# A 3x3 convolution on one core: all inputs through GpSimd's queue, a 20-row head without fp32 staging, and a first store that waits for the fourth pair

## The chip, the cores and the metric

The kernel runs on one core of a Trainium2 chip. The metric is the device time of one execution in microseconds (us), the median of some runs. Most runs of one kernel agree within 0.3% (126.94 to 127.12 us for the kernel before), so differences of half a percent need several runs beside runs of the kernel before on the same chip. Engines go by the profiler's names: PE multiplies matrices (TensorE) and PEld loads its weights, DVE is VectorE, ACT is ScalarE, POOL is GpSimd and SP is Sync. A DMA packet is one piece of a load or store on one of the 16 DMA engines.

## The reference, cut to what matters

```python
batch, c_in, h, w, c_out, k = 16, 64, 64, 64, 128, 3
# x: (16, 64, 64, 64) fp32, weight: (128, 64, 3, 3) fp32, 90% zeros
x_pad = np.pad(x, ((0, 0), (0, 0), (1, 1), (1, 1)))
output[b, co] += weight[co, ci, kh, kw] * x_pad[b, ci, kh:kh+h, kw:kw+w]   # over ci, kh, kw
```

The input is 16.8 MB, the weights are 0.29 MB and the output is 33.6 MB, all fp32. The kernel treats the weights as dense.

## The kernel before

Two images make a pair, whose 2 x 64 channels fill the 128 partitions; there are eight pairs. The products are taken in bf16. The loads on GpSimd's queue turn the inputs into bf16 on their way into the core; only the first 32 rows of pair 0 (the "head") come in fp32 by Sync's queue and are then cast by VectorE and ScalarE. For part of the rows GpSimd adds neighbouring rows first, and PE uses the sum for both ("sums" below). ACT and DVE copy PE's results out ("evacuation").

```python
w_sb = const_pool.tile([C_OUT, C_IN * KH * KW], FP32, name="w_sb")
nc.sync.dma_start(out=w_sb, in_=weight.rearrange("o i kh kw -> o (i kh kw)"))
x_head = o_pool.tile([128, H, W], FP32, name="o")
nc.sync.dma_start(out=x_head[:, 0:HEAD, :], in_=pair(0)[:, 0:HEAD, :])        # HEAD = 32
nc.gpsimd.dma_start(out=xs[0][:, HEAD:H, :], in_=pair(0)[:, HEAD:H, :])
ident = const_pool.tile([128, 128], BF16, name="ident")
make_identity(nc, ident)
def load(p):
    nc.gpsimd.dma_start(out=xs[p], in_=pair(p))
EARLY = 4
for p in range(1, EARLY):
    load(p)
# ... filling matmuls, weight casts and transposes on PE, cast_x of the head's rows ...
for p in range(NP):
    o = [o_pool.tile([C_OUT, H, W], FP32, name="o") for _ in range(2)]         # 7 buffers
    for blk in range(4):
        ...                        # sums on GpSimd, products on PE, evacuation by ACT and DVE
        if p > 0 and blk == 1 and p + EARLY - 1 < NP:
            load(p + EARLY - 1)
    for n in range(2):
        nc.sync.dma_start(out=out[2 * p + n], in_=o[n])                        # last pair: in halves
```

## Time and profile before

| | before |
|---|---|
| time, median of 4 runs | 127.04 us |
| HBM read and written | 17.07 + 33.55 MB |
| first DMA packet, last DMA packet | 1.76, 123.95 us |
| first product of PE, end of its stream of products | 7.43, 111.1 us |
| stores alone, 72 to 114 us | 426 GB/s |

The time is about 3.4 us longer than the end of the last DMA packet in the profiled execution (127.33 against 123.95 us).

### The profile page before, as it was taken

To read this page: it belongs to the slowest core of one execution; us is meant where nothing else is said; L and a number is where in the kernel's file an instruction comes from. 1 tells how busy PE (TensorE), PEld (TensorE's weight loads), DVE (VectorE), ACT (ScalarE), POOL (GpSimd) and SP (SyncE) were. 2 spreads that over 40 slices of the span, in tenths; PEclk is the share of its full clock that TensorE was granted. 3 is DMA by queue.
4 is the path that set the end of the run, shared out by engine and by line. 5 is a ranking of instruction groups with operands and counts; after the bars stand their busy time and mean duration, and the time that the engine had idled before them with its cause. 6 is when DMAs were issued, how large, how long until landed. Compare 5 with 4: busy or idle time off the path is not lost.

```text
span 125.6 us, 2510 instructions
## 1 busy us (share of the span) xinstructions
PE 109.4 (87%) x1014; PEld 56.1 (45%) x1014; DVE 82.3 (66%) x135; ACT 39.0 (31%) x71; POOL 40.6 (32%) x45
## 2 busy tenths in 40 slices
PE   6769999999999999999999999999999999970000
PEld 6624444545454545444554555455545555430000
DVE  0352477877787777888788878877877787772000
ACT  4541533333333333333333333333333333330000
POOL 6327353334433443334333333333333330000000
PEclk9967999999999999999999999999999999999555
DMA  4999999999999999999999999999999999999980
GB/s 119 361 230 214 214 209 219 217 157 399 423 334 305 303 433 311 344 308 407 342 305 329 397 428 444 418 420 423 438 428 444 418 423 423 433 405 423 431 373 26
DMA packets 4044, 42.93 MB, mean 342 GB/s; under 512 B 448, under 2 KB 448, under 8 KB 704
## 3 DMA queue, kind: packets, MB, share of 16 engines
q1 hardware_dynamic: 2880, 34.90, 66.1%
q0 software_dynamic: 1152, 7.86, 30.9%
q8 instruction: 8, 0.13, 0.4%
q14 instruction: 4, 0.03, 0.1%
HBM read 17.07 MB, written 33.55 MB: 403 GB/s over the span
## 4 chain that ended last, share of the span: by engine, by line
PE 83%; DMA 5%; DVE 1%; issue 1%; DVEq 0%; SPq 0%
PE ps L146 83%; DMA o<-in_x_dram 5%; DVE o L179 1%; DVEq L229 0%; DVE x L97 0%; SPq L60 0%; DVEq L179 0%
## 5 line engine op out<-in xcount | busy, mean ns | idle before, releaser
L179 DVE TENSOR_TENSOR o<-ps,pc 128x512 f32<-128x512 f32 x124 | 77.8, 686 | 22.1 <-PE ps L146 19.8
L146 PE MATMUL ps<-x,wT 64*128 64x504 bf16 (+3 forms) x780 | 90.1, 378 | 1.5 <-DVE x L97 1.5
L146 PEld LDWEIGHTS <-wT 64*128 64x128 bf16 x966 | 52.1, 95 | 54.0 <-issue 3.4
L165 POOL TENSOR_TENSOR s<-x 128x512 bf16<-128x512 bf16 x31 | 35.6, 1151 | 59.7 <-PE ps L146 43.3
L172 ACT COPY pc<-ps 128x512 f32<-128x512 f32 x62 | 33.3, 589 | 64.0 <-issue 61.8
L146 PE MATMUL ps<-s,wT 64*128 64x512 bf16 (+1 forms) x186 | 25.5, 377 | 0.0
L82 PE MATMUL ps<-idle_rhs 128*128 128x128 bf16 x39 | 3.9, 283 | 1.0 <-DVE idle_rhs L77 1.0
L82 PEld LDWEIGHTS <-idle_rhs 128*128 128x128 bf16 x39 | 3.5, 133 | 1.0 <-DVE idle_rhs L77 1.0
L68 POOL DMA_DIRECT2D x<-in_x_dram x7 | 3.9, 559 | 0.0
L160 DVE COPY o<-ps 128x512 f32<-128x512 f32 x2 | 1.4, 692 | 3.6 <-PE ps L146 3.6
L101 DVE CAST w_bf<-w_sb 128x192 bf16<-128x192 f32 (+1 forms) x4 | 1.1, 345 | 2.8 <-DMA w_sb<-in_weight_dram 2.8
L159 ACT COPY o<-ps 128x512 f32<-128x512 f32 x2 | 1.2, 586 | 4.0 <-PE ps L146 4.0
L97 ACT CAST x<-o 128x576 bf16<-128x576 f32 (+1 forms) x2 | 1.5, 802 | 1.2 <-DMA o<-in_x_dram 1.2
L97 DVE CAST x<-o 128x576 bf16<-128x576 f32 x1 | 0.5, 460 | 2.0 <-DMA o<-in_x_dram 2.0
L101 ACT ACT_TABLE_LOAD x1 | 1.3, 1283 | 0.7 <-PEq L218 0.7
L101 ACT CAST w_bf<-w_sb 128x64 bf16<-128x64 f32 (+1 forms) x2 | 0.7, 416 | 1.7 <-DMA w_sb<-in_weight_dram 1.7
L107 PE MATMUL ps<-ident,w_bf 128*128 128x128 bf16 x9 | 0.9, 222 | 0.3 <-DVE w_bf L101 0.3
L111 DVE TENSOR_TENSOR wT<-ps,wT 128x384 bf16<-128x384 f32 x2 | 1.0, 550 | 0.0
L63 POOL DMA_DIRECT2D x<-in_x_dram x1 | 0.7, 691 | 0.8 <-POOLq L218 0.8
L107 PEld LDWEIGHTS <-w_bf 128*128 128x128 bf16 x9 | 0.5, 97 | 0.8 <-DVE w_bf L101 0.7
L77 DVE MEMSET idle_rhs<- 128x64 uint32 x1 | 0.1, 112 | 0.8 <-PEq L218 0.8
L122 DVE CAST wT<-ps 128x384 bf16<-128x384 f32 x1 | 0.6, 552 | 0.0
(8 smaller groups left out, 1.9 us busy)
## 6 DMA issues: line engine op xcount, KB each, us to landing
out_dram<-o SPq DMA_DIRECT2D x14, 2048.0 KB, 16.9
x<-in_x_dram POOLq DMA_DIRECT2D x7, 1024.0 KB, 15.5
out_dram<-o SPq DMA_DIRECT2D x4, 1024.0 KB, 10.6
o<-in_x_dram SPq DMA_DIRECT2D x1, 1024.0 KB, 5.7
x<-in_x_dram POOLq DMA_DIRECT2D x1, 512.0 KB, 7.5
w_sb<-in_weight_dram SPq DMA_DIRECT2D x1, 288.0 KB, 3.0
```

The lines of the kernel that those rows point to most:

```text
L68: nc.gpsimd.dma_start(out=xs[p], in_=pair(p))
L82: nc.tensor.matmul(idle_ps, idle_rhs, idle_rhs, start=True, stop=True)
L97: copy(out=xs[0][:, a:b, :], in_=x_head[:, a:b, :])
L101: copy(out=w_bf4[:, g, a:b, :], in_=w_v[:, k : k + b - a, :])
L107: nc.tensor.matmul(wps[:, j, :], src, ident, start=True, stop=True)
L111: nc.vector.tensor_tensor(out=wT[:, g], in0=wps, in1=wT[:, G1], op=SUB)
L146: nc.tensor.matmul(ps[n][:, lo:hi, c_lo:c_hi], tap(g, kw, n), src[q, a:b:step, c_lo + kw - 1 : c_hi + kw - 1], start=(i == 0), stop=(i == ...
L159: nc.scalar.copy(out=o[0][:, r0 : r0 + rows, :], in_=ps[0])
L160: nc.vector.tensor_copy(out=o[1][:, r0 : r0 + rows, :], in_=ps[1])
L165: nc.gpsimd.tensor_tensor(out=s, in0=xs[p][:, r0 : r0 + 16 : 2, :], in1=xs[p][:, r0 + 1 : r0 + 16 : 2, :], op=ADD)
L172: nc.scalar.copy(out=c, in_=shared[n])
L179: nc.vector.tensor_tensor(out=o[n][:, first : r0 + 16 : 2, :], in0=ps[n], in1=pc[n], op=ADD)
```

## The change

The intent is to put all inputs in one queue in the order in which they are needed, to do without the fp32 staging and its casts, to start PE sooner on a shorter head, and to keep the first stores from competing with the loads that PE needs.

```diff
-    HEAD = 32
+    HEAD = 20
...
+    def load(p, a=0, b=H):
+        return nc.gpsimd.dma_start(out=xs[p][:, a:b, :], in_=pair(p)[:, a:b, :])
     w_sb = const_pool.tile([C_OUT, C_IN * KH * KW], FP32, name="w_sb")
     nc.sync.dma_start(out=w_sb, in_=weight.rearrange("o i kh kw -> o (i kh kw)"))
-    x_head = o_pool.tile([128, H, W], FP32, name="o")
-    nc.sync.dma_start(out=x_head[:, 0:HEAD, :], in_=pair(0)[:, 0:HEAD, :])
-    nc.gpsimd.dma_start(out=xs[0][:, HEAD:H, :], in_=pair(0)[:, HEAD:H, :])
+    load(0, 0, HEAD)
     ident = const_pool.tile([128, 128], BF16, name="ident")
     make_identity(nc, ident)
...
-    EARLY = 4
-    for p in range(1, EARLY):
-        load(p)
+    load(0, HEAD, H)
+    EARLY = 5
+    landed = [load(p) for p in range(1, EARLY)][-2]
...   (cast_x and its three calls go)
-                if p > 0 and blk == 1 and p + EARLY - 1 < NP:
-                    load(p + EARLY - 1)
+                if p > 1 and blk == 1 and p + EARLY - 2 < NP:
+                    load(p + EARLY - 2)
...
-                nc.sync.dma_start(out=out[2 * p + n], in_=o[n])
+                st = nc.sync.dma_start(out=out[2 * p + n], in_=o[n])
+                if p == n == 0:
+                    tc.add_manual_dep(st.ins, landed.ins.name, ..., reason="loads first")
```

More of the change, by code (lines that the diff above doesn't have):

```diff
@@ L58 @@
     xs = [x_pool.tile([128, H, W], BF16, name=f"x{p}") for p in range(NP)]
+    def load(p, a=0, b=H):
+        return nc.gpsimd.dma_start(out=xs[p][:, a:b, :], in_=pair(p)[:, a:b, :])
     w_sb = const_pool.tile([C_OUT, C_IN * KH * KW], FP32, name="w_sb")
     nc.sync.dma_start(out=w_sb, in_=weight.rearrange("o i kh kw -> o (i kh kw)"))
-    x_head = o_pool.tile([128, H, W], FP32, name="o")
-    nc.sync.dma_start(out=x_head[:, 0:HEAD, :], in_=pair(0)[:, 0:HEAD, :])
-    nc.gpsimd.dma_start(out=xs[0][:, HEAD:H, :], in_=pair(0)[:, HEAD:H, :])
+    load(0, 0, HEAD)
     ident = const_pool.tile([128, 128], BF16, name="ident")
     make_identity(nc, ident)
-    def load(p):
-        nc.gpsimd.dma_start(out=xs[p], in_=pair(p))
-    EARLY = 4
-    for p in range(1, EARLY):
-        load(p)
+    load(0, HEAD, H)
+    EARLY = 5
+    landed = [load(p) for p in range(1, EARLY)][-2]
     idle_rhs = const_pool.tile([128, 128], BF16, name="idle_rhs")
@@ L94, in tap @@
         return wT[64 * n : 64 * n + 64, g, (kw - n) % 3, :]
-    def cast_x(copy, a, b):
-        copy(out=xs[0][:, a:b, :], in_=x_head[:, a:b, :])
     def cast(g, copy, a, b):
@@ L118 @@
     cast(G2, nc.vector.tensor_copy, 3, 4)
-    cast_x(nc.vector.tensor_copy, 0, 9)
     nc.scalar.copy(out=wT[:, G1], in_=transposed(G1))
@@ L125 @@
     keep_busy(12)
-    cast_x(nc.scalar.copy, 9, 18)
     difference(G01, ps0)
     difference(G21, ps2)
-    cast_x(nc.scalar.copy, 18, HEAD)
     def product(terms, rows):
@@ L202 @@
             for n in range(2):
-                nc.sync.dma_start(out=out[2 * p + n], in_=o[n])
+                st = nc.sync.dma_start(out=out[2 * p + n], in_=o[n])
+                if p == n == 0:
+                    tc.add_manual_dep(
+                        st.ins,
+                        landed.ins.name,
+                        mybir.DependencyInfo(
+                            mybir.DependencyClass.Sync, mybir.DependencyReason.DATA
+                        ),
+                        reason="loads first",
+                    )
 _INS = ['x', 'weight']
```

## The prediction

> **What bounds the kernel now.** I read the page first, from its slices, then the queues, then the chain of waits.
>
> ```profile
> PE   6769999999999999999999999999999999970000
> DMA  4999999999999999999999999999999999999980
> GB/s 119 361 230 214 214 209 219 217 157 399 423 334 305 303 433 311 344 308 407 342 305 329 397 428 444 418 420 423 438 428 444 418 423 423 433 405 423 431 373 26
> ...
> q1 hardware_dynamic: 2880, 34.90, 66.1%
> q0 software_dynamic: 1152, 7.86, 30.9%
> ...
> HBM read 17.07 MB, written 33.55 MB: 403 GB/s over the span
> ...
> PE 83%; DMA 5%; DVE 1%; issue 1%; DVEq 0%; SPq 0%
> ```
>
> The chain names PE for 83%, and PE is solid from the third slice on. But PE ends four slices before the span does, while the DMA engines are at 9 from the second slice to the second last. A load that converts is counted by the bf16 bytes that land, half of what is read from HBM, so the 214 of the load phase is 428 of reading. Nowhere is there a slack slice on the DMA. So the chain, which stops at the last store, hides the bound: all 16 DMA engines, 66.1 + 30.9 = 97% of the span in the two data queues.
>
> The windows view gives the rates (columns: window, its us, five engines' busy us, clock, DMA share, GB/s):
>
> ```profile
> 24.00:26.00 2.00, 2.00 (x22) 1.03 (x20) 1.40 (x4) 0.44 (x1) 0.62 (x1) 1.00 1.15 205
> 26.00:28.00 2.00, 2.00 (x22) 0.96 (x18) 1.27 (x3) 1.07 (x2) 1.15 (x1) 1.00 0.93 131
> ...
> 72.00:114.00 42.00, 40.30 (x379) 19.98 (x374) 32.65 (x53) 13.39 (x26) 11.05 (x10) 1.00 1.00 426
> 114.00:122.00 8.00, 0.00 (x0) 0.00 (x0) 0.00 (x0) 0.00 (x0) 0.00 (x0) 0.66 0.98 416
> ```
>
> Stores alone run at 426 GB/s. All 50.62 MB at that rate take 118.8 us. The first packet starts near 1.76 us and the last ends near 124 us, so only some 3.4 us of the DMA's stretch are not full-rate transfer: a ragged end of about 1.5 us, a ramp of about half a microsecond at the start, and one dip. The dip is at 24 to 28 us, where the first store enters: the loads' 215 falls to 205 and then 131, and the packets there are twice as long. In 26 to 28 us about 0.9 us of transfer is lost, with the neighbours 1.1 us.
>
> The timeline of the start (start, us, engine, line, what):
>
> ```profile
> 0.74 0.38 SPq L60 DMA_DIRECT2D w_sb<-in_weight_dram  x1
> ...
> 1.18 0.43 SPq L62 DMA_DIRECT2D o<-in_x_dram  x1
> 1.24 0.69 POOL L63 DMA_DIRECT2D x<-in_x_dram  x1 [0.80 <-POOLq L218]
> ...
> 6.92 0.46 DVE L97 CAST x<-o 128x576 bf16<-128x576 f32 x1 [2.02 <-DMA o<-in_x_dram]
> 7.29 0.55 DVE L122 CAST wT<-ps 128x384 bf16<-128x384 f32 x1
> 7.43 5.57 PE L146 MATMUL ps<-x,wT 64*128 64x512 bf16 x36 [1.53 <-DVE x L97]
> ```
>
> PE's first useful product waits until 7.43 us for a cast of the fp32 head, and PE ends its stream at 111.1 us.
>
> **What the Trainium skill says.** Page "DMA: Bandwidth & Descriptors", section "Issuing engines are not separate DMA queues": all issuers share the same 16 engines and interleave. The trace agrees: where both queues are busy the landed stores plus twice the landed loads stay near 428 GB/s. So moving the head from one queue to the other makes no bandwidth. Same page, "Specifications": the first byte takes about 1 us on GpSimd's path, 0.6 us on Sync's. Here the weight load's issue ends at 1.12 us and its first packet starts at 1.76 us, 0.64 us later: agrees. GpSimd's first load is issued at 1.24 us, and its first packet starts only at 5.18 us, 3.9 us later; that seems to contradict the page. Page "Perfetto Trace Analysis", section "DMA Instruction — SWDGE (GPSIMD)": the recorded instruction ends when the last descriptor has been written. Then these descriptors were ready at 1.93 us, and something else held them.
>
> **What held them** is the hinge of this prediction. In the packets, every engine moves its 8 weight packets, its 8 packets of the fp32 head, and then at once, with no gap, its first packet of GpSimd's queue. A late doorbell would have left gaps, or would have cut in between head packets. So GpSimd's packets stood behind work already taken in. The first store looks the same from the other side: issued at 23.5 us, first packet 27.7 us, 4.2 us later, on the queue that needed 1.0 us from the start of the issue when nothing was ahead. I conclude that about 3 us of either delay is what is already in the engines, and that alone, behind only 0.29 MB of weights, GpSimd's first packet starts at 1.93 + 0.7 to 1.0, about 2.7 us.
>
> **The change part by part.**
> 1. *Start of the DMA's stream.* Removed: a 1.05 MB load on Sync's queue. Added: the same bytes on GpSimd's. HBM bytes: unchanged, 50.62 MB. What can change is a hole between weights and head. The weights are finished on the engines between 2.9 and 3.3 us. First packet at 2.7 us: no hole; at 3.5 us: a hole of about 0.4 us; at 5.2 us, if the delay were fixed: about 2.0 us (5.2 less 3.2). Added packet cost: a converting packet of 8 KB takes 322 ns against 309 ns for a plain one, 8 per engine: 0.1 us. I take +0.3 us in all.
> 2. *Start of PE.* The first 20 rows are 0.66 MB; with 0.29 MB of weights 0.95 MB, at 426 GB/s 2.2 us. From an effective start of 2.5 us that is 4.7, plus 0.4 us to the semaphore (head's last packet 6.5 us, cast 6.9 us): 5.1 us. The cast of 0.46 us goes, and so does the wait of the weight cast behind it at 7.29 us. Now the weights' own chain decides: the filling products end at 5.89 us. The weights may land up to 0.4 us later as they share with the head. PE starts at 5.9 to 6.4, about 1.3 us earlier, and its stream ends near 109.8 instead of 111.1 us.
> 3. *The other 44 rows* are 1.44 MB, 3.4 us more: landed near 8.7 us. GpSimd's sum for the second block needs them, takes 1.15 us, and ends near 10 us; PE wants it 5.4 us after its start, at 11.3 us or later. No stall.
> 4. *The store's wait.* Pair 3 was issued at 3.54 us and landed 20.6 us later, at 24.1 us; the first store went at 23.5 us. In the new kernel the bytes up to pair 3 are the same, so it lands near 24.2 us and the store goes some 0.7 us later than before, beside pair 4, which is already queued. The engines have 4.9 us of pair 4 to do meanwhile (2.10 MB at 426), longer than the 4.2 us until a store's first packet. So there is no hole, and the dip stays about as it is. I credit 0.1 us of it.
> 5. *Output buffers.* The head took one of 7. Every pair still waits for the store seven allocations earlier. No PE wait for a store is seen now, and a store stream moved by under 1 us makes none.
> Sum: +0.3 - 0.1 = +0.2 us, so 127.2 us. The 1.3 us of PE is off the path that sets the end: the queue is already some 10 us behind when PE stops (last evacuation 113.7 us, last packet 124 us).
>
> **The rivals.**
> A. *GpSimd's first-packet delay is fixed at about 4 us.* For: 3.9 us here, and about 4.1 us for loads issued at 43.8 and 56.6 us. Against: all had full engines ahead of them, and the store shows the same delay. Then the DMA stands for 2.0 us after the weights, the whole stream moves by that, PE starts near 7.3 as now, and the time is 129.0 to 129.4 us.
> B. *PE sets the end.* For: 83% of the chain, idle only at the start. Then all 1.3 us arrive at the end: 125.7 us. Against: 10 us of transfers after PE's end at full rate.
> C. *The wait cures the dip*: loads are nearly done when stores enter, 1.1 us of transfer comes back, 126.0 us. Against: pair 4 is as much in the way as before.
> D. *Six loads outstanding at the start instead of four* block GpSimd's queue and make its sums late. For: only the four were tried here. Against: PE has slack of over 1 us there and the DMA would run on. About 127.5 us.
>
> **Range and chances.** My own path has 0.65, A in full or in part 0.18, C 0.10, B and D the rest. Centre 127.2 us; range 126.1 to 128.9 us, longer upwards because of A. Faster by 2% needs under 124.5 us, which is less than the ragged end and the dip together can give: 0.03. Slower by 2% needs over 129.6 us, rival A and a hole at the store besides: 0.07. Within 2%: 0.90.
>
> **What would show it right or wrong.** In the new profile: DMA share 9 from the second slice on and the first packet of the software queue before 3.3 us (step 1; rival A if it is after 4.5 us, with a hole in 3 to 5 us); first product on L140 or so at 5.9 to 6.4 us (step 2); no wait of PE for the sums up to 15 us (step 3); first store issued at 24 to 24.6 us, and the 131 GB/s dip 4 us later still there (step 4); no PE wait for stores (step 5); PE's stream over by 110 us and yet the same last packet near 124 us. Wrong altogether would be an end that moves with PE's end, or a mixed phase whose rate differs from 426.

## More of the kernel before

The start of the windows view is needed later (columns: window in us, its length, busy us and instructions of PE, PEld, DVE, ACT and POOL, granted clock, DMA share, GB/s landed); a load that converts lands half of the bytes that it reads, so some 215 is full speed for GpSimd's loads, and some 428 for Sync's.

```profile
3.00:4.00 1.00, 1.00 (x10) 0.79 (x8) 0.24 (x1) 0.24 (x2) 1.00 (x3) 1.00 1.08 413
4.00:5.00 1.00, 0.66 (x9) 0.46 (x9) 0.90 (x4) 0.81 (x3) 0.09 (x1) 1.00 0.94 393
5.00:6.00 1.00, 0.90 (x16) 0.81 (x14) 0.00 (x0) 0.64 (x2) 0.00 (x0) 1.00 0.99 303
6.00:7.00 1.00, 0.00 (x0) 0.00 (x0) 0.08 (x1) 0.08 (x1) 0.00 (x0) 1.00 1.13 225
```

In 3 to 5 us it is Sync's head that lands at about 400, in 5 to 6 us the two queues change over, and from 6 us on GpSimd's loads land at full speed at once.

## The result

| | before | changed |
|---|---|---|
| median | 127.04 us (126.94 to 127.12, 4 runs) | 128.44 us (128.21 to 128.75, 4 runs) |
| ratio of the fast runs | | 1.0112, 95% interval 1.0089 to 1.0136 |
| last DMA packet, profiled execution | 123.95 us | 125.22 us |

A ratio is the mean time of one kernel's fast runs over that of the other's of the same rounds, so it is not quite the ratio of the medians quoted. Executions over 1.5% slower than the fastest of the same kernel are left out of the means. The change costs 1.1%. That is inside the range and within 2%, but 1.2 us above the predicted 127.2 us, and the sign matters to whoever would keep the change.

The page of the changed kernel, the lines that answer to those of before:

```profile
PE   6876999999999999999999999999999999910000
DMA  4999999999999999999999999999999999999960
GB/s 101 129 199 216 225 212 220 212 230 390 405 310 323 336 418 305 312 341 429 315 318 323 421 424 439 436 413 429 434 434 423 423 424 449 423 400 424 424 269 10
...
q1 hardware_dynamic: 2736, 33.85, 63.3%
q0 software_dynamic: 1296, 8.39, 32.8%
HBM read 17.07 MB, written 33.55 MB: 399 GB/s over the span
```

The DMA engines are "busy" just as before, and as many bytes cross HBM. But the second slice landed 129 GB/s. A busy share counts the time that packets take, and slow packets look as busy as quick ones; only the GB/s row beside it shows the loss. The dip that the kernel before has in its ninth slice (157) is gone: the changed kernel has 230 there.

The start of the timeline:

```profile
0.74 0.38 SPq L65 DMA_DIRECT2D w_sb<-in_weight_dram  x1
...
1.24 0.69 POOL L61 DMA_DIRECT2D x<-in_x_dram  x1 [0.79 <-POOLq L221]
...
2.46 2.68 POOL L61 DMA_DIRECT2D x<-in_x_dram  x5
...
7.03 3.99 PE L140 MATMUL ps<-x,wT 64*128 64x512 bf16 x36 [0.90 <-DMA x<-in_x_dram]
...
10.83 3.36 POOL L159 TENSOR_TENSOR s<-x 128x512 bf16<-128x512 bf16 x3 [5.70 <-DMA x<-in_x_dram]
...
12.03 0.82 PE L140 MATMUL ps<-s,wT 64*128 64x512 bf16 x6 [1.01 <-POOL s L159]
```

PE waits for the head until 7.03 us, and then 1.01 us more for GpSimd's sum of the second block, whose rows landed late. Its stream ends at 110.3 us, 0.8 us sooner than before, while the kernel ends later. The windows view of the changed kernel says where the transfers were slow:

```profile
3.00:4.00 1.00, 1.00 (x10) 0.79 (x8) 0.26 (x1) 0.27 (x2) 1.00 (x3) 1.00 0.91 162
4.00:5.00 1.00, 0.77 (x8) 0.55 (x8) 0.89 (x4) 0.65 (x3) 1.00 (x3) 1.00 1.35 134
5.00:6.00 1.00, 1.00 (x17) 0.96 (x15) 0.77 (x2) 0.78 (x2) 0.14 (x1) 1.00 0.80 93
6.00:7.00 1.00, 0.14 (x3) 0.09 (x1) 0.72 (x2) 0.00 (x0) 0.00 (x0) 1.00 0.77 144
...
26.00:28.00 2.00, 2.00 (x22) 1.06 (x20) 1.27 (x3) 0.80 (x2) 0.97 (x1) 1.00 1.05 221
```

Between 4 and 7 us 134, 93 and 144 landed where 215 is full speed. At 26 to 28 us 221 landed where the kernel before had 131. So the two kernels lose transfer time in different places.

**A ledger of lost transfer.** From the packets I summed, for each half microsecond, the HBM bytes that moved, and took what was missing against 428 GB/s as time lost, from 1.5 us on; it includes the wait for the first packet at 1.74 to 1.76 us. To find each engine's last packet I followed the packets from end to start, as the records do not name the engine. Each row is one profiled execution. All in us:

| kernel | time, median | lost by 10 us | lost 22 to 31 us (first stores) | mean of the 16 engines' last packets | the last of them |
|---|---|---|---|---|---|
| before | 127.04 | 1.02 | 1.16 | 122.40 | 123.95 |
| changed | 128.44 | 2.56 | 0.02 | 122.76 | 125.22 |
| e1 no wait | 128.24 | 2.64 | 0.31 | 123.06 | 124.84 |
| e2 head by Sync | 126.82 | 1.67 | 0.10 | 121.92 | 123.46 |
| e3 before + wait | 127.25 | 1.02 | 0.91 | 122.09 | 123.80 |
| e4 one load fewer ahead | 127.98 | 2.64 | 0.01 | 122.89 | 124.53 |
| e5 head 32 rows | 128.61 | 2.10 | 0.17 | 122.48 | 124.91 |
| e6 before + ahead + wait | 127.06 | 1.07 | 0.59 | 122.00 | 123.63 |
| e7 contiguous head | 128.65 | 2.91 | -0.01 | 123.25 | 125.02 |
| e8 pair 0 in one load | 130.24 | 2.09 | 0.12 | 125.32 | 126.87 |
| e9 loads held back | 128.12 | 2.30 | 0.07 | 122.51 | 124.65 |
| e10 filler on Sync | 128.56 | 1.58 | 0.10 | 123.48 | 125.04 |
| e11 before, 20 rows | 127.11 | 1.47 | 0.53 | 122.13 | 123.68 |
| e12 out of step | 127.22 | 1.20 | 0.53 | 122.18 | 124.04 |

The sum checks: changed against before, +1.54 at the start and -1.14 at the first stores are +0.40 us, and the mean of the last packets moved by +0.36 us. The rest is that the slowest engine is 2.46 us behind the mean instead of 1.55, which adds 0.91 us: 125.22 - 123.95 = 1.27 us. In all fourteen profiled executions the time is 3.2 to 3.5 us more than the last packet, so it is the slowest of the sixteen engines that counts. The profiled execution of the changed kernel is its slowest run (128.75 us), so part of the 0.91 us is that run's own. How far one execution can be trusted shows where kernels share a part: with one and the same start the loss repeats (1.02, 1.02 and 1.07 in before, e3 and e6; 2.56, 2.64 and 2.64 in the changed kernel, e1 and e4), and so does the dip with the wait and a 20-row head on GpSimd's queue (0.02, 0.01, -0.01 and 0.07 in the changed kernel, e4, e7 and e9). The lag of the slowest engine does not repeat in these four: 2.46, 1.64, 1.77 and 2.14 us.

How the slowest engine comes to lag shows in the DMA view cut to 118 to 126 us, 0.2 us a column. Of before:

```profile
GB/s 328 492 410 410 492 369 451 451 410 369 532 369 410 451 410 451 410 369 164 287 328 164 287 82 0 41 41 0 41 0 0 0 0 0 0 0 0 0 0 0
```

and of the changed kernel:

```profile
GB/s 451 369 492 451 369 410 451 451 410 451 410 451 328 451 532 287 410 451 328 328 369 287 123 246 123 82 123 0 41 41 0 41 0 41 41 0 0 0 0 0
```

Each kernel fades out from about 121.5 us on, as engine after engine is done, and one engine alone moves the last packets (41 GB/s is one packet of 8 KB in a column); in the changed kernel it does so for longer.

### The profile page after: what moved, and what is told of

Same layout as the page of the kernel before. It is cut to its first block, busy times and chain, and to the rows that moved or that the text cites. A ratio compares the mean times of both kernels' runs of the same rounds, so it can differ in the third digit from the quotient of the medians.

```text
span 126.9 us, 2507 instructions
## 1 busy us (share of the span) xinstructions
PE 108.4 (85%) x1014; PEld 59.5 (47%) x1014; DVE 81.9 (65%) x134; ACT 37.4 (30%) x69; POOL 41.1 (32%) x46
## 4 chain that ended last, share of the span: by engine, by line
PE 77%; DMA 6%; POOL 2%; issue 1%; DVE 1%; DVEq 0%; POOLq 0%
PE ps L140 77%; DMA x<-in_x_dram 6%; DVE o L173 1%; POOL s L159 1%; POOL x L61 1%; DVEq L232 0%; POOL ident masks.py:199 0%; POOL ident masks.py:197 0%; POOLq masks.py:199 0%; POOLq L159 0%; POOLq L221 0%; DVEq L173 0%
## 5 line engine op out<-in xcount | busy, mean ns | idle before, releaser
L140 PE MATMUL ps<-x,wT 64*128 64x504 bf16 (+3 forms) x780 | 88.8, 373 | 0.9 <-DMA x<-in_x_dram 0.9
L140 PEld LDWEIGHTS <-wT 64*128 64x128 bf16 x966 | 55.1, 94 | 49.9 <-DVE o L154 1.3
L61 POOL DMA_DIRECT2D x<-in_x_dram x9 | 5.1, 574 | 0.8 <-POOLq L221 0.8
L116 ACT CAST wT<-ps 128x384 bf16<-128x384 f32 x1 | 0.5, 478 | 0.4 <-PE ps L104 0.4
L120 ACT CAST wT<-ps 128x384 bf16<-128x384 f32 x1 | 0.5, 478 | 0.2 <-PE ps L104 0.2
```

Source lines behind the costliest of these rows:

```text
L61: return nc.gpsimd.dma_start(out=xs[p][:, a:b, :], in_=pair(p)[:, a:b, :])
L140: nc.tensor.matmul(ps[n][:, lo:hi, c_lo:c_hi], tap(g, kw, n), src[q, a:b:step, c_lo + kw - 1 : c_hi + kw - 1], start=(i == 0), stop=(i == ...
```

## The experiments

Three calls of up to four kernels and one of a single kernel, twelve kernels in all. Each call ran beside the kernel before on the same chip: medians 127.17, 127.06, 127.17 and 127.27 us there. The changed kernel itself ran in a call of its own (127.04 us there), so differences to it of 0.2 us or so say little. e1 to e4 were written to tell the parts of the change apart. **Theory 1** was that the start loses the time and the store's wait gives back the dip; the rivals were that the wait itself costs (2), that the dip's absence was chance (3), or that the number of loads queued ahead matters (4).

### e1: the changed kernel without the wait

```diff
-                if p == n == 0:
-                    tc.add_manual_dep(st.ins, landed.ins.name, ..., reason="loads first")
```

> The changed kernel without the first store's wait. Theory 1 (the 1.4 us come from the start, where GpSimd's queue alone feeds the engines and loses about 1.3 us between 4 and 7 us, and the wait gives back the 1.1 us dip that the early first store made): first store near 22 us, the dip of packets twice as long is back near 24 to 28 us, and the time rises to 129.2 to 129.7 us. Theory 2 (the wait itself costs, the store stream starts late): the time falls to 127.0 to 127.6 us. Theory 3 (the wait does nothing, the dip's absence is chance): 128.3 to 128.6 us.

Measured: 128.24 us (127.97 to 128.36). The first store went at 23.13 instead of 25.38 us. The start is as slow as ever (2.64 us lost). The dip came back only to 0.31 us, not to 1.1. Theory 2 falls, as the time did not drop to 127.6 or less. Theory 1 is right on the start and wrong on the wait: the wait is worth about 0.3 us of transfer at the mean, and nothing that the times show. Something else in the change had removed most of the dip.

### e2: the head by Sync's queue again, the rest as changed

```diff
-    load(0, 0, HEAD)
+    x_head = o_pool.tile([128, H, W], FP32, name="o")
+    nc.sync.dma_start(out=x_head[:, 0:HEAD, :], in_=pair(0)[:, 0:HEAD, :])
+    load(0, HEAD, H)
...
+    cast_x(nc.vector.tensor_copy, 0, 9)
...
+    cast_x(nc.scalar.copy, 9, HEAD)
```

> The changed kernel, but the 20 head rows go through Sync's queue in fp32 with casts, as before; loads ahead and wait kept. Theory 1: no stall at 4 to 7 us and no dip at 24 to 28 us, so better than both: 125.9 to 126.5 us. Theory 2 (the wait costs): stays near 128.4 us. Theory 4 (the stall is of six loads queued ahead, whoever loads the head): a stall is still seen at 4 to 8 us and the time stays at 127.5 us or more.

Measured: 126.82 us (126.71 to 126.93), 1.6 us below the changed kernel by this one edit. The windows view of e2:

```profile
4.00:5.00 1.00, 0.75 (x11) 0.53 (x11) 0.83 (x4) 0.81 (x2) 0.61 (x2) 1.00 1.14 279
5.00:6.00 1.00, 0.83 (x15) 0.74 (x13) 0.00 (x0) 0.57 (x2) 0.00 (x0) 1.00 0.90 187
6.00:7.00 1.00, 0.37 (x4) 0.22 (x5) 0.89 (x3) 0.78 (x1) 0.00 (x0) 1.00 1.04 214
...
26.00:28.00 2.00, 2.00 (x22) 1.08 (x20) 2.00 (x4) 0.24 (x1) 0.14 (x1) 1.00 1.06 221
```

By 6 us GpSimd's loads land at full speed (214), and there is no dip (221). The loss by 10 us fell from 2.56 to 1.67 us, not to the 1.02 of before. Theory 4 falls here too: five loads are written on GpSimd's queue by 4.6 us, and yet its stream is at full speed by 6 us. The time is 0.3 us above the upper end of what I had expected (126.5 us). e2 is the quickest kernel: each of its four runs is below each of the seven runs of before (127.01 us and up), though the interval of the ratio, 0.9931 (0.9856 to 1.0007), is wide because two runs of before came out at 128.7 us.

### e3: the kernel before with the wait alone

```diff
-    for p in range(1, EARLY):
-        load(p)
+    landed = [load(p) for p in range(1, EARLY)][-1]
...   (and the wait of the first store on `landed`)
```

> The kernel before, with only the first store's wait for the fourth pair added. Theory 1: the dip at 25 to 28 us shrinks or goes, and the time falls by up to 1.1 us: 126.0 to 126.6 us. Theory 2: 127.5 us or more. Theory 3: 127.0 us with the dip still there.

Measured: 127.25 us median of four runs, fast runs 127.18 to 127.28 and a slow one of 129.37 us. The first store went at 24.34 instead of 23.50 us, and the windows view of e3 has the dip still:

```profile
24.00:26.00 2.00, 2.00 (x22) 1.10 (x20) 1.59 (x3) 0.24 (x1) 0.42 (x1) 1.00 1.04 213
26.00:28.00 2.00, 2.00 (x22) 1.03 (x18) 1.27 (x3) 1.08 (x2) 1.16 (x1) 1.00 1.00 135
```

It only starts later and is a quarter smaller (0.91 against 1.16 us). Theory 3 is nearest: the wait alone does not pay.

### e4: one load fewer ahead

```diff
-    EARLY = 5
-    landed = [load(p) for p in range(1, EARLY)][-2]
+    EARLY = 4
+    landed = [load(p) for p in range(1, EARLY)][-1]
...
-                if p > 1 and blk == 1 and p + EARLY - 2 < NP:
-                    load(p + EARLY - 2)
+                if p > 0 and blk == 1 and p + EARLY - 1 < NP:
+                    load(p + EARLY - 1)
```

> The changed kernel with pairs 1 to 3 ahead instead of 1 to 4, so five loads written at the start instead of six, the fifth pair's in the loop as before. Theory 1: nothing changes, 128.2 to 128.7 us, stall at 4 to 7 us as long. Theory 4 (number of loads queued ahead, or their descriptors being written beside the transfers): the stall is shorter and the time 127.3 to 127.9 us.

Measured: 127.98 us (127.74 to 128.08), between the two theories' numbers. The loss at the start is 2.64 us as in e1, so the load less does not shorten it; the slowest engine lags by 1.64 us here. The number of loads ahead is not the cause.

The next four ask what is slow about the head. **Theory Q**: GpSimd's loads start badly with nothing ahead of them. **Theory P**: pieces of 5 KB cut out of rows of 16 KB are slow to read, by either queue.

### e5: 32 rows instead of 20

```diff
-    HEAD = 20
+    HEAD = 32
```

> The changed kernel with 32 head rows instead of 20, still by GpSimd's queue. In the changed kernel packets took 1.2 us per engine too long between 3 and 7 us. Theory Q (the queue: GpSimd's loads start badly when nothing is ahead of them): the loss stays at 1.0 us or more, time 128.0 to 128.7 us. Theory P (the piece: 5 KB out of every 16 KB row are slow to read, whoever reads them): 8 KB pieces are as quick as they were before, loss 0.4 us or less, time 126.7 to 127.3 us.

Measured: 128.61 us with a wide scatter (127.77 to 129.03). Lost by 10 us: 2.10 us, 0.46 less than with 20 rows, but still 1.08 more than before, with the same 32 rows by Sync. Packets alone took some 0.8 us per engine too long between 3 and 7 us. The time is Q's; the piece's size has a part in it.

### e6: 32 rows by Sync, with loads ahead and the wait

```diff
-    HEAD = 20
+    HEAD = 32
...   (against e2; the head's last rows are cast as before)
```

> 32 head rows by Sync in fp32 as before, but pairs 1 to 4 ahead and the first store's wait, as in the change: it differs from e2 in the 20 rows only, and from e3 in the fourth load's place. Theory P: start as quick as before (loss from 3 to 7 us under 0.3 us against 0.8 in e2). The dip at the first store was 1.16 us before, 0.83 in e3, 0.17 in e2: if it hangs on the fifth load being issued early it is under 0.3 us here and the time is 126.2 to 126.6 us; if it hangs on the 32 rows (engines in step with each other) it is 0.7 us or more and the time 127.0 to 127.3 us.

Measured: 127.06 us (127.01 to 127.66). The start is as quick as before (1.07 us), as P expects of the larger pieces. The dip is 0.59 us, between both expectations: the early fifth load takes 0.3 us off e3's dip, the 20 rows another 0.5. So the wait, the early load and the shorter head each soften the dip, and the head most; the first store goes at 24.49 us here and at 24.50 in e2, so its time is not what differs between the two.

### e7: the same bytes in the same pieces, but contiguous (a wrong result)

```diff
-    load(0, 0, HEAD)
+    flat = x.rearrange("n i h w -> (n i h) w")[0 : 128 * HEAD, :]
+    nc.gpsimd.dma_start(out=xs[0][:, 0:HEAD, :], in_=flat.rearrange("(p h) w -> p h w", h=HEAD))
```

> The changed kernel, whose first load takes as many bytes in the same 128 pieces of 5 KB, but from one contiguous stretch of x: a wrong result on purpose. Theory P (gaps between the pieces, every 16 KB): no loss in the head's own packets, loss from 3 to 7 us 0.5 us or less, time 127.0 to 127.6 us. Theory Q: as the changed kernel, 1.0 us or more and 128.1 to 128.7 us.

Measured: 128.65 us (128.45 to 128.86), 2.91 us lost by 10 us. The gaps between the pieces are not the cause. P falls in this form.

### e8: pair 0 in one load of 64 rows

```diff
-    HEAD = 20
+    HEAD = 64
...
-    load(0, HEAD, H)
```

> The changed kernel with pair 0 in one load of 64 rows by GpSimd's queue: no pieces at all, contiguous 2 MB. PE starts 1.5 us later, near 8.5 us, which is off the path. Theory P: no loss from 3 to 7 us, time 126.6 to 127.2 us. Theory Q: the loss of 1.0 us or more is still there, time 128.0 us or more.

Measured: 130.24 us (129.93 to 130.64). Lost by 10 us: 2.09 us, as in e5, though there are no pieces at all. So GpSimd's start costs 1.07 us more than before whatever the shape (2.10 and 2.09 against 1.02), and Q stands. The time itself went beyond what either theory said, because my expectation of PE was wrong. The chain of e8 (start, us, what):

```profile
1.24 9.73 DMA x<-in_x_dram
...
11.01 104.16 PE ps L139 x954
```

The last engine brought pair 0 at 10.67 us, and PE began at 11.01 instead of 8.5 us. The windows view then shows the engines at a share of 0.88 and 369 GB/s in 102 to 108 us, and summed as for the ledger 2.6 us are lost between 31 and 110 us (0.04 in the changed kernel): stores came too late to keep them busy. PE's slack is real, but 4 us is more than there is.

### e9: fewer descriptors written beside the first transfers

```diff
-    landed = [load(p) for p in range(1, EARLY)][-2]
+    load(1)
+    hold = const_pool.tile([128, 1, 4], BF16, name="hold")
+    nc.gpsimd.tensor_copy(out=hold, in_=xs[0][:, 0:1, 0:4])
+    landed = [load(p) for p in range(2, EARLY)][-2]
```

> The changed kernel, but GpSimd issues the loads of pairs 2 to 4 only once the head has landed (it reads four elements of it first), so that three loads are written at the start instead of six. Theory D (the slow packets of 3 to 7 us come from GpSimd writing further loads' descriptors beside them, 2.5 to 5.1 us): the landed rate from 4 to 7 us, 134, 93 and 144 GB/s in the changed kernel, rises to 180 or more, time 127.2 to 127.7 us. Theory R (a stream of GpSimd's loads with nothing ahead of it needs some 4 us to come to speed, whatever is issued behind): rates as in the changed kernel, 128.0 to 128.7 us.

Measured: 128.12 us (127.51 to 128.19). The windows view of e9:

```profile
4.00:5.00 1.00, 1.00 (x14) 0.79 (x14) 0.80 (x4) 0.71 (x2) 0.00 (x0) 1.00 1.01 124
5.00:6.00 1.00, 0.64 (x12) 0.56 (x10) 1.00 (x3) 0.48 (x1) 0.00 (x0) 1.00 0.93 176
6.00:7.00 1.00, 0.74 (x8) 0.42 (x9) 0.33 (x1) 0.00 (x0) 0.73 (x3) 1.00 0.91 175
```

The rates of 5 to 7 us rose from 93 and 144 to 176 and 175, but 4 to 5 us stayed at 124, after GpSimd had stopped writing at 3.5 us; and when the held loads were written (6.4 to 8.0 us) some 0.3 us were lost between 7.5 and 9 us. In all 0.26 us less was lost. That is the net: by the packets 0.5 us less was lost from 3 to 7 us, and 0.3 us more from 7 to 9.5 us, where the writing now was. So the writing (D) may cost up to a third of the 1.54 us where it falls, though a load written at 18.16 us in the kernel before, into the full stream, left the packets there at 624 to 625 ns. The rest, the slow start itself (R), is what remains.

### e10: a filler on Sync's queue

```diff
+    filler = const_pool.tile([128, HEAD, W], FP32, name="filler")
+    nc.sync.dma_start(out=filler, in_=pair(7)[:, 0:HEAD, :])
     load(0, 0, HEAD)
```

> The changed kernel with an extra load of 0.66 MB on Sync's queue behind the weights, into a tile that nobody reads: bytes for 1.54 us at 426 GB/s more. Theory R: while the filler keeps the engines busy, GpSimd's loads come to speed unseen, so the loss of 1.3 us shrinks to 0.3 to 0.8 us and the time is 128.9 to 129.5 us, clearly less than 1.54 us above the changed kernel. If the loss belongs to the bytes or pieces themselves and not to the queue's start: 129.9 us or more.

Measured: 128.56 us (128.31 to 129.13), ratio to before 1.0112, exactly that of the changed kernel, with 0.66 MB more to move. The windows view of e10:

```profile
4.00:5.00 1.00, 0.69 (x10) 0.47 (x10) 0.89 (x4) 0.81 (x3) 1.00 (x3) 1.00 0.97 271
5.00:6.00 1.00, 0.89 (x16) 0.80 (x14) 0.91 (x2) 0.63 (x2) 0.14 (x1) 1.00 1.03 207
6.00:7.00 1.00, 0.00 (x0) 0.00 (x0) 0.57 (x2) 0.00 (x0) 0.00 (x0) 1.00 1.19 234
```

GpSimd's loads, unchanged in order and issue, now land at 207 and 234 from 5 us on. Bytes for 1.54 us were nearly free: the loss by 10 us fell from 2.56 to 1.58 us, and with the filler's own 1.54 us the mean last packet moved by 0.72 us. The rest of the bill is the slowest engine's, which lags by 1.56 us here and by 2.46 in the changed kernel's profile. The time came out 0.3 us below the range expected. This speaks for theory R: what is slow is the start of GpSimd's stream while nothing else keeps the engines busy, and not its bytes or pieces. GpSimd's first packet comes at 4.69 us here, behind the filler, against 2.96, and its packets of 5 KB read then take 209 to 225 ns nearly all the time, with 0.01 us lost in each half microsecond from 5.5 to 7 us; in the changed kernel packets of that size took up to 1134 ns.

### e11: the kernel before with 20 rows

```diff
-    HEAD = 32
+    HEAD = 20
...   (the head's last rows are cast in one call instead of two)
```

> The kernel before with 20 head rows on Sync's queue instead of 32, nothing else. It tells what of e2's 126.8 us is the 20 rows. If the shorter head takes the engines out of step and so softens the dip at the first store (e2: 0.17, e6 with 32 rows: 0.62 us): dip under 0.5 us against 1.16 before, loss from 3 to 7 us about 0.7 us as in e2, time 126.7 to 127.1 us. If the wait or the early fifth load did it in e2: dip 0.8 us or more and 127.3 us or more.

Measured: 127.11 us (127.02 to 127.17), ratio 0.9992 (0.9964 to 1.0020). Lost at the start 1.47 us, 0.45 more than with 32 rows; lost at the first stores 0.53 us, 0.63 less, with no wait and no early load. The two cancel. So the shorter head costs half a microsecond at the start on either queue (2.56 against 2.10 on GpSimd's) and softens the dip by about as much. Two cautions: PE starts sooner here and the first store goes 2.2 us earlier (21.31 us), so in this run the dip had two changes; and e10 ran pieces of the same size without loss once the stream was going, so the size costs only at the start.

### e12: engines pushed out of step

```diff
+    for k in (12, 8, 4):
+        step = const_pool.tile([128, 16, W], FP32, name=f"step{k}")
+        nc.sync.dma_start(out=step[0:k], in_=pair(7)[0:k, 0:16, :])
...   (against e6)
```

> e6 (32 rows by Sync, pairs 1 to 4 ahead, wait) with three tiny extra loads of 12, 8 and 4 rows of 4 KB behind the head, into tiles that nobody reads, meant to put the 16 DMA engines out of step by 0, 0.15, 0.3 and 0.45 us; 98 KB more, 0.2 us at the mean. In all runs so far the dip at the first store was 0.5 to 1.2 us where the middle twelve engines ended the fourth pair within 0.6 us of each other (before, e3, e6, e11) and 0.3 us or less where they were 0.7 us or more apart. Theory S (the dip is of engines in step): spread over 0.6 us, dip under 0.3 us against 0.59 in e6, mean last packet near 121.8 us, time 126.5 to 127.0 us. Otherwise (spread is only a companion of it): dip 0.5 us or more, 127.1 to 127.5 us.

Measured: 127.22 us (127.06 to 127.41), dip 0.53 us against 0.59 in e6. Inconclusive: the edit put fifteen engines 0.5 us apart at the end of the fourth pair (22.85 to 23.38 us) instead of 0.4, short of the 0.6 that I had asked for. What the dip hangs on stays open.

## Why the prediction was right or wrong

**The bound** was right. The end follows the last DMA packet in every run, within 3.2 to 3.5 us. PE's stream ended 0.8 us sooner and the kernel 1.4 us later, which rules out rival B.

**The hinge** was right: with only the weights ahead, GpSimd's first packet came at 2.96 us (2.7 predicted), so most of the 3.9 us of before was the queue of work in the engines. e10 shows it once more: with the filler ahead the first packet is back at 4.69 us. Rival A is ruled out as stated, with its fixed delay of about 4 us. Yet what A feared, a start whose bytes come late, came by another way.

**Step 1 failed**: "I take +0.3 us in all". It summed a hole and a slower packet and took for granted that a stream whose first packet is early is at full speed at once; and it reckoned with packets of 8 KB, though 20 rows make pieces of 5 KB. Measured, the start loses 1.54 us more than before, 1.24 us above the term. Of that 1.07 us belongs to GpSimd's stream starting with nothing beside it (e5 and e8, and hidden again in e10), and about 0.5 us to the head's smaller pieces, which cost as much on Sync's queue (e11). Why the stream is slow to start was not shown; descriptors written at the same time explain 0.26 us net and at most some 0.5 us (e9). The sign named for this step, a DMA share of 9 from the second slice and a first packet before 3.3 us, came true and yet could not see the failure: the rate was what to ask for.

**Step 2** was wrong in size: PE began its products at 7.03 us instead of 5.9 to 6.4, as the last engine brought the head only at 6.67 us. **Step 3** was wrong too: PE waited 1.01 us for the second block's sum. Neither reached the end.

**Step 4 failed** in the other direction: "the dip stays about as it is. I credit 0.1 us of it". It went from 1.16 to 0.02 us, and the store went at 25.38 us instead of 24 to 24.6, as the fourth pair landed late. But rival C, that the wait cures it, is not right either: the wait alone took 0.25 us off (e3) and its removal gave 0.3 us back (e1). The shorter head took more (0.63 us in e11, 0.49 us between e6 and e2). So the misses of steps 1 and 4 nearly cancelled at the mean of the engines, +0.40 us against a predicted +0.2. That was luck, as neither had been foreseen. It was luck too that 128.44 us lies in the range of 126.1 to 128.9: its upper part stood there for rival A, which did not happen.

**Missing from the sum** was that the lag of the slowest engine can change; the prediction had it as a fixed ragged end of 1.5 us. The slowest was 1.55 us behind the mean before and 2.46 us in the changed kernel's profile: 0.91 of the 1.27 us between the two profiles, and so, by these two profiles, the larger part of what the centre was low by. The stall at the start was uneven (the head's completions spread over 2.1 us, against 0.5 us for pair 0's first load of GpSimd's before), but e1 and e4 have as uneven a start (2.1 and 1.9 us) and lags of 1.8 and 1.6 us, so that the one causes the other is not shown. **Step 5** held: no PE wait for a store appears. Rival D held in so far as PE did wait; the count of loads was not its cause (e4).

## What to carry to other kernels

In a kernel bound by transfers, look at the rate of the first microseconds, and try to fill them from the queue that starts quickly while the converting queue comes to speed behind it: here putting the head back on Sync's queue took 1.6 us off (e2). That leaves e2 only 0.2 to 0.4 us below the kernel before, within its interval. Read the GB/s row beside the DMA share, since slow packets count as busy, and ask when the slowest engine ends, not the average one. The wait that orders loads before stores was worth at most 0.3 us of transfer here, and nothing in the time (e1, e3).

## What the Trainium skill lacked or had wrong

- Page "DMA: Bandwidth & Descriptors", section "Issuing engines are not separate DMA queues", says that issuing from several engines "will only save the time on the sequencer it takes to initiate the DMA". At the start that was not all: the same 20 rows by Sync's instead of GpSimd's queue took 1.6 us off the kernel (126.82 against 128.44 us), and 0.66 MB added on Sync's queue ahead of GpSimd's cost about 0.1 us of time instead of 1.54 (128.56 against 128.44 us; 0.72 us at the mean of the engines).
- The same page, section "Specifications", gives first-byte times. With only the weights ahead they agree if they are counted from the end of the issue (GpSimd: about 1 us on the page; descriptors written at 1.93 us, first packet at 2.96 us, 1.0 us later); from its start at 1.24 us it is 1.7 us. It lacks that a stream then runs below full speed for some 4 us: 134, 93 and 144 GB/s landed from 4 to 7 us where 215 is full.
- No page that I read gives a measured time for the delay behind work already in the engines: 3.9 us from issue to first packet for GpSimd's first load and 4.2 us for Sync's first store, both in the kernel before (2.9 us for the first store of the changed kernel, 25.38 to 28.24 us).
- No page that I read has the loss when stores first enter a stream of loads: 1.16 us in the kernel before, 0.0 to 0.9 us in the others, on a cause that these runs leave open.
- Page "Perfetto Trace Analysis", section "Identifying the Most-Contended Engine", warns that 16 engines make the DMA's occupancy misleading. These runs add a number to watch: the slowest engine ended 1.5 to 2.5 us after the mean, in every profile, and differed by up to 0.8 us between kernels with the same kind of start (1.64 us in e4, 2.46 us in the changed kernel).
